# Layer 1 of a two-layer decoder trunk: the softmax of head groups 0 and 2 turned by DMA in 16-bit halves, that of groups 1 and 3 by PE transposes

## The chip, the cores and the metric

The kernel runs on one core of a Trainium2 chip. The metric is the device time of one execution in microseconds; the text compares the median of several runs. The engines are TensorE (PE; its weight loads are shown apart as PEld), VectorE (DVE), ScalarE (ACT), GpSimd (POOL) and SyncE (SP). SP computes nothing here, it issues DMAs. Every engine and every queue works through its own instructions in a fixed order, and waits on semaphores where one instruction needs the result of another engine.

## The reference

A sequence of 256 tokens of width 2048 goes through two layers and a last RMSNorm. A layer is: RMSNorm, mixer, residual add, RMSNorm, SwiGLU, residual add. Layer 0 mixes with sliding-window attention beside an mLSTM. Layer 1, the one that is changed, mixes with forgetting attention: 16 heads of 128, causal softmax with a bias made of a running sum of log forget gates. Everything is float32. Cut to what matters here:

```python
def forgetting_attention_mixer(xn, w_in, b_f, w_out):
    q, k, v, f = split_cols(xn @ w_in, FOX_SIZES)          # 3 x 2048 and 16 columns
    q, k, v = to_heads(q), to_heads(k), to_heads(v)        # 16 heads of 128
    log_f = log_sigmoid(f + b_f)
    c = cumsum(log_f, axis=1)
    def one_block(qb, cb, pb):                             # 128 queries
        s = einsum('bhqd,bhkd->bhqk', qb, k) * scale
        s = s + cb[..., None] - c[:, :, None, :]
        s = where(pb[:, None] >= k_pos[None, :], s, -inf)
        p = softmax(s, axis=-1)
        return einsum('bhqk,bhkd->bhqd', p, v)
    out = map(one_block, blocks of 128 queries)
    return concat_heads(out) @ w_out
```

## The kernel before

All weights stream from HBM once. A chunk is two 128-row blocks of up to 512 columns (512 KB). It is loaded by SP into one of four buffers `raw` (L113), rounded by ACT to a shorter float format (`hi`, L174), and DVE makes the remainder (`lo = raw - hi`, L175). There are six buffers each for `hi` and `lo`. The activations are split likewise (`xh`, `xl`, and `mh`, `ml` for the mixer's output), and each product is three matmuls: hi x hi, hi x lo, lo x hi (L205 to L207 in `gemm`, L441 to L443 in `three`). A chunk is twelve matmuls of 512 columns.

`pair_group` (L448) multiplies two 512-column groups of weights at a time in eight positions, given as (kind, pair). Kind 0 is plain: two chunks, 24 matmuls. Kind 1 is mixed: it forms sums and differences of the two weight blocks on DVE (L500 to L503), splits them (L311, L312), and needs 21 matmuls. `MIX` has the mixed positions 1, 3 and 5. The products of the mixed positions go to four PSUM banks of the pool `pm` and are put together by `combine` (L455) ahead of the last position. A callback `inner` is called there too, after `combine`; callbacks in `todo` are called at the position that stands with each (`run_due`, L185), and what they put on ACT is queued behind the latest cast of a weight chunk.

Layer 1 goes through four head groups `i` of four heads (L1053). For each, `pair_nat(i)` projects q and k, `project` makes a 512-column group of v, and `attention` (L333) does scores, bias, mask, maximum, exponential and division. The scores stand in one tile `s` of 128 x 4 heads x 384 columns: 128 columns for the first block of queries, which sees one block of keys, and 256 for the second, which sees two. `attention` ends with the division (L385) and returns the function `rest`; that is passed as `inner` to the next group's `pair_nat`, so that group i's `rest` is issued ahead of the last position of `pair_nat(i+1)`. Group 3's `rest` is called after the loop.

`rest` turns the 12 blocks of 128 x 128 so that keys lie on partitions: eight PE transposes to PSUM (L394) and two ACT copies to the tile `t0` (L395), four transposes (L398) and one DVE copy to `t1` (L399). Then come the value matmuls (L402, L403) and the split of their result into `mh` and `ml` (L412, recorded at L311 and L312). The output projection reads `mh` and `ml` as its stationary side, group after group.

For i < 3 the function `turn` (L1017) turns q and k by DMA: ACT parts float32 numbers into two planes of upper and lower 16-bit halves (L1022), SP issues four DMA transposes of 128 x 512 halves for each of q and k (L1025), and a `join` later puts the halves together again on ACT (L1030). For i = 3 q and k are turned by PE (L330).

The order of the instructions on each engine comes from a scheduler at compile time. It runs a model of the time of all engines and issues what is ready there, in the order of the program where there is a choice. On the chip that order is fixed.

The sums of x for the mixed positions of layer 1 are made in the first group's `pair_nat`, at positions 1, 3 and 6 (`sums_of_x`, L1034), in the tiles `t0` and `t1`, which the attention doesn't use yet. Layer 0's attention uses the same function `attention`, with tiles of its own pool.

Of the kernel before, what the change touches and what calls it, by code (L numbers as in the profile page):

```python
# [7 lines left out]
F32 = mybir.dt.float32  # L8
BF16 = mybir.dt.bfloat16
F32R = mybir.dt.float32r  # L10
U16 = mybir.dt.uint16
# [6 lines left out]
P = 128  # L18
D = 2048
S = 256  # L20
# [3 lines left out]
NB = 512  # L24
# [6 lines left out]
FOX_H, FD = 16, 128  # L31
# [12 lines left out]
MIX = ((0, 0), (1, 1), (0, 2), (1, 3), (0, 4), (1, 5), (0, 6), (0, 7))  # L44
MIX0 = ((0, 0), (0, 1), (0, 2), (1, 3), (0, 4), (1, 5), (0, 6), (0, 7))
# [4 lines left out]
LATER = (6, 10, 3, 5)  # L50
LATER_DOWN = (5, 6)
RAWS = 4
PARTS = (0, 3, 7, 11)


# [7 lines left out]
def trunk(  # L63
# [20 lines left out]
    nc = tc.nc  # L84

    sp_ = ctx.enter_context(tc.tile_pool(name="split", bufs=1))
    xh = sp_.tile([P, KT, S], F32R, name="xh")
    xl = sp_.tile([P, KT, S], F32R, name="xl")
# [151 lines left out]
    def whole(hi, lo, pair):  # L240
        ks = slice(2 * pair, 2 * pair + 2)
        return lambda full: nc.vector.tensor_tensor(
            out=full, in0=hi[:, ks, :].bitcast(F32), in1=lo[:, ks, :].bitcast(F32), op=ALU.add
        )

    def sums_of(pool, sh, sl, copies, full=None, tags=("tmp", "tmp"), bufs=None):
        if full is None:
            full = pool.tile([P, 2, NT, P], F32, tag=tags[0], name="full", bufs=bufs)
            copies(full.rearrange("p i t q -> p i (t q)"))
        s = pool.tile([P, 4, P], F32, tag=tags[1], name="s4", bufs=bufs)  # L250
        nc.vector.tensor_tensor(out=s[:, 0, :], in0=full[:, 0, 1, :], in1=full[:, 1, 1, :], op=ALU.add)
        nc.vector.tensor_tensor(out=s[:, 1, :], in0=s[:, 0, :], in1=full[:, 0, 0, :], op=ALU.subtract)
        nc.vector.tensor_tensor(out=s[:, 2, :], in0=full[:, 0, 0, :], in1=full[:, 0, 1, :], op=ALU.subtract)
        nc.vector.tensor_tensor(out=s[:, 3, :], in0=full[:, 1, 0, :], in1=s[:, 1, :], op=ALU.subtract)
        split_plain(sh, sl, s)
# [74 lines left out]
            nc.tensor.transpose(pt[:, i, :], s_, ident)  # L330
        nc.vector.tensor_copy(dst, pt[:, 0:m, :])

    def attention(sp, q_of, k_of, v_of, dv, scale, bias0, bias1, k_tile, sinks=None, negc=None, s_bufs=2, causal=False):  # L333
        s = sp.tile([P, 4, 3 * P], F32, tag="s", name="s", bufs=s_bufs)
        for b, cols, bias in ((0, P, bias0), (1, S, bias1)):
            pq = [pm.tile([P, 2, cols], F32, tag="pm", name=f"p{b}") for _ in range(2)]
            for j in range(4):
                nc.tensor.matmul(pq[j % 2][:, j // 2, :], q_of(j, b), k_of(j)[:, 0:cols], start=True, stop=True)  # L338
            for half in range(2):
                hs = slice(half, 4, 2)  # L340
                nc.vector.scalar_tensor_tensor(
                    out=s[:, hs, b * P : b * P + cols],
                    in0=pq[half],
                    scalar=scale,
                    in1=bias[:, hs, :],
                    op0=ALU.mult,
                    op1=ALU.add,
                )
            if causal and b == 0:
                o = s[:, :, 0:P]  # L350
                nc.gpsimd.affine_select(
                    out=o, in_=o, pattern=[[0, 4], [-1, P]], compare_op=ALU.is_ge, fill=NEG, base=0, channel_multiplier=1
                )
        parts = (slice(0, P), slice(P, 3 * P))
        mx = sm.tile([P, NT, 4], F32, tag="mx", name="mx")
        for b in range(NT):
            nc.vector.reduce_max(mx[:, b, :], s[:, :, parts[b]], axis=AX)
        neg = sm.tile([P, NT, 4], F32, tag="neg", name="neg")
        den = sm.tile([P, NT, 4], F32, tag="den", name="den")
        if sinks is not None:  # L360
            sk = sinks[:, None, :].broadcast_to([P, NT, 4])
            nc.vector.tensor_tensor(out=mx, in0=mx, in1=sk, op=ALU.max)
            nc.vector.tensor_scalar(neg, mx, -1.0, None, op0=ALU.mult)
        else:
            nc.vector.tensor_tensor(out=mx, in0=mx, in1=negc, op=ALU.subtract)
            nc.vector.scalar_tensor_tensor(
                out=neg, in0=negc, scalar=-1.0, in1=mx, op0=ALU.mult, op1=ALU.subtract
            )
        for b in range(NT):
            for j in range(4):  # L370
                e = s[:, j, parts[b]]
                nc.scalar.activation(
                    e, e, AF.Exp, bias=neg[:, b, j : j + 1], accum_out=den[:, b, j : j + 1]
                )
        if sinks is not None:
            es = sm.tile([P, NT, 4], F32, tag="es", name="es")
            nc.vector.tensor_tensor(out=es, in0=neg, in1=sk, op=ALU.add)
            nc.scalar.activation(es, es, AF.Exp)
            nc.vector.tensor_tensor(out=den, in0=den, in1=es, op=ALU.add)
        rec = sm.tile([P, NT, 4], F32, tag="rec", name="rec")  # L380
        nc.vector.reciprocal(rec, den)
        for b in range(NT):
            for j in range(4):
                e = s[:, j, parts[b]]
                nc.vector.tensor_scalar(e, e, rec[:, b, j : j + 1], None, op0=ALU.mult)  # L385
        def rest():
            t0 = sp.tile([P, 4, S], F32, tag="t0", name="t0", bufs=1)
            t1 = sp.tile([P, 4, P], F32, tag="t1", name="t1", bufs=1)
            for half in range(2):
                pt = pm.tile([P, 2, S], F32, tag="pm", name="pp")  # L390
                for jj in range(2):
                    j = 2 * half + jj
                    for b in range(NT):
                        nc.tensor.transpose(pt[:, jj, b * P : (b + 1) * P], s[:, j, b * P : (b + 1) * P], ident)  # L394
                nc.scalar.copy(t0[:, 2 * half : 2 * half + 2, :], pt)  # L395
            pt = pm.tile([P, 4, P], F32, tag="pm", name="pp1")
            for j in range(4):
                nc.tensor.transpose(pt[:, j, :], s[:, j, 2 * P : 3 * P], ident)  # L398
            nc.vector.tensor_copy(t1, pt)  # L399

            def pv(po, j):
                nc.tensor.matmul(po, v_of(j, 0), t0[:, j, :], start=True, stop=False)  # L402
                nc.tensor.matmul(po[:, P : 2 * P], v_of(j, 1), t1[:, j, :], start=False, stop=True)  # L403

            per = P // dv
            for q in range(0, 4 // per, 2):
                po = pm.tile([P, 2, S], F32, tag="pm", name="po")
                for i in range(2):
                    for u in range(per):
                        pv(po[u * dv : (u + 1) * dv, i, :], (q + i) * per + u)  # L410
                ks = slice(k_tile + q, k_tile + q + 2)
                split_plain(mh[:, ks, :], ml[:, ks, :], po)  # L412

        return rest

    def spare_halves():
        return [
# [245 lines left out]
    with tc.tile_pool(name="ev", bufs=1) as ev:  # L663
# [17 lines left out]
        sx = [hs_[:, i, :, :, :] for i in range(2)]  # L681
# [4 lines left out]
        vs = sw.tile([P, NT, nk], F32, name="vs")  # L686
# [75 lines left out]
        pu = pm.tile([P, NB], F32, tag="pm", name="pu")  # L762
# [77 lines left out]
        with tc.tile_pool(name="mp", bufs=1) as mp:  # L840
# [20 lines left out]
            c = pair_even(OFF_QM, OFF_KM, MIXQ)  # L861
# [35 lines left out]
            c = pair_even(OFF_OM, OFF_VM, MIXV)  # L897
# [62 lines left out]
    with tc.tile_pool(name="od", bufs=1) as od:  # L960
        sx = [od.tile([P, NX, 4, P], F32R, name=f"sx{i}") for i in range(2)]
# [70 lines left out]
            return join  # L1032

        def sums_of_x(j, pair):  # L1034
            return lambda: sums_of(od, sx[0][:, j, :, :], sx[1][:, j, :, :], whole(xh, xl, pair), tags=("t0", "t1"))

        todo = [(p, sums_of_x(j, pair)) for p, j, pair in [(1, 1, 3), (3, 2, 5), (6, 0, 1)]]

# [5 lines left out]
        def pair_nat(c0, c1, todo=(), order=MIX, inner=None):  # L1044
            plain, c = pair_group(od, 0, x_of, sums_x, [(wi1, c0), (wi1, c1)], order, todo, halves, inner)
            for m in range(2):
                for t in range(NT):
                    o = c[:, 2 * m + t, :]
                    nc.vector.tensor_tensor(out=o, in0=plain[m][t], in1=o, op=ALU.add)
            return c  # L1050

        rest, vs = None, []
        for i in range(4):  # L1053
            qt = od.tile([P, 4, S], F32, tag="qt", name="qtf")
            kt = od.tile([P, 4, S], F32, tag="kt", name="ktf")
            c = pair_nat(i * NB, FOX_H * FD + i * NB, todo if i == 0 else (), MIX if i else MIX0, rest)
            for a in range(2 * NT):
                nc.scalar.mul(c[:, a, :], c[:, a, :], r1[:, a % NT : a % NT + 1])
            for m, dst in enumerate((qt, kt)):
# [21 lines left out]
            def v_of(j, b, i=i, vn=vs[i]):  # L1081
                if i == 3 and j >= 2:
                    return vtail[:, b, (j - 2) * FD : (j - 1) * FD]
                return vn[:, b, j * FD : (j + 1) * FD]
# [11 lines left out]
                negc=negc[:, :, 4 * i : 4 * i + 4],  # L1096
                s_bufs=1,
                causal=i < 3,
            )
        rest()  # L1100


# [74 lines left out]
```

## Time and profile before

| | us |
|---|---|
| median of 3 runs | 2098.47 |
| lowest and highest | 2097.71, 2098.72 |
| the profiled execution, its time | 2098.21 |
| the profiled execution, its span | 2096.5 |
| softmax of group 0 divided (L385), start | 1145.73 |
| softmax of group 2 divided (L385), start | 1284.10 |

The span goes from the first to the last instruction of the profiled execution; positions in microseconds are counted from its start. The granted clock of TensorE is 0.998 of full speed. A row of the timeline gives start, length, engine, line, operation, output and input tiles, shape and count; in square brackets stands the idle time of the engine just before and what ended it. A row of a line's view gives the least, the median and the greatest length in nanoseconds, then the first and the last start.

### The profile page before, as it was taken

To read this page: it belongs to the slowest core of one execution; us is meant where nothing else is said; L and a number is where in the kernel's file an instruction comes from. 1 tells how busy PE (TensorE), PEld (TensorE's weight loads), DVE (VectorE), ACT (ScalarE), POOL (GpSimd) and SP (SyncE) were. 2 spreads that over 40 slices of the span, in tenths; PEclk is the share of its full clock that TensorE was granted. 3 is DMA by queue.
4 is the path that set the end of the run, shared out by engine and by line. 5 is a ranking of instruction groups with operands and counts; after the bars stand their busy time and mean duration, and the time that the engine had idled before them with its cause. 6 is when DMAs were issued, how large, how long until landed. Compare 5 with 4: busy or idle time off the path is not lost.

```text
span 2096.5 us, 27042 instructions
## 1 busy us (share of the span) xinstructions
PE 2079.4 (99%) x9559; PEld 1727.5 (82%) x9559; DVE 1831.4 (87%) x2416; ACT 1348.6 (64%) x1709; POOL 40.2 (2%) x68
## 2 busy tenths in 40 slices
PE   8999999999999999999999999999999999999998
PEld 7888888888888888888888888888888888888886
DVE  5688868999999998999898778679999999999994
ACT  6665559665567655766676666587655667456753
POOL 2000000000000000000000000000000000000000
PEclk9999999999999999999999999999999999999999
DMA  7455558666566666666576756486756567666663
GB/s 243 141 181 181 201 147 277 229 199 213 199 197 228 220 205 215 206 217 203 183 212 211 236 160 195 151 264 214 223 190 223 194 199 246 206 202 207 222 198 136
DMA packets 290600, 428.31 MB, mean 204 GB/s; under 512 B 89016, under 2 KB 97312, under 8 KB 290336
## 3 DMA queue, kind: packets, MB, share of 16 engines
q1 hardware_dynamic: 288896, 421.27, 63.3%
q0 software_dynamic: 1520, 5.30, 0.8%
q8 instruction: 75, 1.23, 0.2%
q14 instruction: 61, 0.50, 0.1%
q10 hardware_dynamic: 48, 0.02, 0.0%
HBM read 406.05 MB, written 2.11 MB: 195 GB/s over the span
## 4 chain that ended last, share of the span: by engine, by line
PE 98%; ACT 1%; DMA 1%; issue 0%; DVE 0%; DVEq 0%; POOLq 0%; POOL 0%; ACTq 0%
PE acc L442 21%; PE acc L443 21%; PE acc L441 21%; PE acc L205 6%; PE acc L206 6%; PE acc L207 6%; PE prod L442 5%; PE prod L441 5%; PE prod L443 5%; PE p L338 1%; PE po L402 1%; DMA raw<-in_w_in_odd_dram 0%; PE pp L394 0%; PE ptm L330 0%; PE po L403 0%
## 5 line engine op out<-in xcount | busy, mean ns | idle before, releaser
L174 ACT CAST hi<-raw 128x1024 fp32r<-128x1024 f32 (+3 forms) x655 | 665.8, 1031 | 463.6 <-PE acc L443 286.3
L175 DVE TENSOR_TENSOR lo<-raw,hi 128x1024 fp32r<-128x1024 f32 (+3 forms) x655 | 775.0, 1198 | 144.4 <-ACT hi L174 142.2
L442 PE MATMUL acc<-lo,xh 128*128 128x512 f32 x1254 | 488.8, 390 | 0.5 <-DVE lo L175 0.5
L441 PE MATMUL acc<-hi,xh 128*128 128x512 f32 x1254 | 486.5, 390 | 0.0
L443 PE MATMUL acc<-hi,xl 128*128 128x512 f32 x1254 | 484.9, 390 | 0.0
L442 PEld LDWEIGHTS acc<-lo,xh 128*128 128x128 f32 x1254 | 235.5, 188 | 50.1 <-DVE lo L175 1.2
L443 PEld LDWEIGHTS acc<-hi,xl 128*128 128x128 f32 x1254 | 235.4, 188 | 48.8
L441 PEld LDWEIGHTS acc<-hi,xh 128*128 128x128 f32 x1254 | 235.2, 188 | 48.7 <-issue 0.2
L442 PE MATMUL acc<-lo,mh 128*128 128x512 f32 x437 | 169.7, 389 | 0.0
L443 PE MATMUL acc<-hi,ml 128*128 128x512 f32 x437 | 168.2, 389 | 0.0
L441 PE MATMUL acc<-hi,mh 128*128 128x512 f32 x437 | 167.9, 389 | 0.0
L311 ACT CAST hi<-raw 128x512 fp32r<-128x512 f32 x109 | 67.6, 621 | 93.9 <-PE acc L443 79.0
L206 PE MATMUL acc<-lo,mh 128*128 128x512 f32 x320 | 125.7, 393 | 0.0
L205 PE MATMUL acc<-hi,mh 128*128 128x512 f32 x320 | 125.2, 393 | 0.1
L207 PE MATMUL acc<-hi,ml 128*128 128x512 f32 x320 | 122.3, 393 | 0.0
L311 ACT CAST ht<-t 128x1024 fp32r<-128x1024 f32 x95 | 99.8, 1051 | 34.4 <-PE prod L443 27.8
L312 DVE TENSOR_TENSOR lt<-t,ht 128x1024 fp32r<-128x1024 f32 x95 | 115.8, 1219 | 5.3 <-ACT ht L311 5.3
L311 ACT CAST ht<-raw 128x1024 fp32r<-128x1024 f32 x95 | 99.6, 1049 | 28.3 <-PE acc L443 13.8
L312 DVE TENSOR_TENSOR lt<-raw,ht 128x1024 fp32r<-128x1024 f32 x95 | 115.8, 1219 | 1.3 <-ACT ht L311 1.3
L205 PE MATMUL acc<-hi,xh 128*128 128x512 f32 (+3 forms) x288 | 100.1, 351 | 0.9 <-ACT hi L174 0.9
L206 PE MATMUL acc<-lo,xh 128*128 128x512 f32 (+3 forms) x288 | 100.8, 351 | 0.0
L207 PE MATMUL acc<-hi,xl 128*128 128x512 f32 (+3 forms) x288 | 99.2, 349 | 0.0
(353 smaller groups left out, 3448.7 us busy)
## 6 DMA issues: line engine op xcount, KB each, us to landing
raw<-in_w_gate_dram SPq DMA_DIRECT2D x176, 512.0 KB, 4.4
raw<-in_w_up_dram SPq DMA_DIRECT2D x176, 512.0 KB, 4.6
raw<-in_w_down_dram SPq DMA_DIRECT2D x176, 512.0 KB, 5.1
raw<-in_w_in_odd_dram SPq DMA_DIRECT2D x88, 512.0 KB, 5.3
raw<-in_w_in_even_dram SPq DMA_DIRECT2D x52, 512.0 KB, 4.5
raw<-in_w_out_even_dram SPq DMA_DIRECT2D x32, 512.0 KB, 4.4
raw<-in_w_out_odd_dram SPq DMA_DIRECT2D x32, 512.0 KB, 4.3
hr<-in_w_in_even_dram SPq DMA_DIRECT2D x12, 512.0 KB, 5.3
```

Source lines behind the costliest of these rows:

```text
L174: latest[0] = nc.scalar.copy(hi[:, :, 0:n], raw[:, :, 0:n])
L175: nc.vector.tensor_tensor(out=lo[:, :, 0:n], in0=raw[:, :, 0:n], in1=hi[:, :, 0:n].bitcast(F32), op=ALU.subtract)
L205: nc.tensor.matmul(o, ah[:, ts], hi, start=(k == 0), stop=False)
L206: nc.tensor.matmul(o, ah[:, ts], lo, start=False, stop=False)
L207: nc.tensor.matmul(o, al[:, ts], hi, start=False, stop=(k == k_all - 1))
L311: nc.scalar.copy(dst_h, src)
L312: nc.vector.tensor_tensor(out=dst_l, in0=src, in1=dst_h.bitcast(F32), op=ALU.subtract)
L338: nc.tensor.matmul(pq[j % 2][:, j // 2, :], q_of(j, b), k_of(j)[:, 0:cols], start=True, stop=True)
L402: nc.tensor.matmul(po, v_of(j, 0), t0[:, j, :], start=True, stop=False)
L441: nc.tensor.matmul(o, ah, hi, start=start, stop=False)
L442: nc.tensor.matmul(o, ah, lo, start=False, stop=False)
L443: nc.tensor.matmul(o, al, hi, start=False, stop=stop)
```

## The change

In layer 1, `attention` is called with `turned` for groups 0 and 2. It then issues `turn_p` directly behind the division: ACT parts the 1536 columns of `s` into two planes of 16-bit halves in the tile `tt`, SP issues six DMA transposes of 128 x 512 halves from `tt` back into `s`, and a function `join` is returned, which puts the halves together into `tt` by two ACT copies. The join is handed to the next group's `pair_nat` as a callback at position 4 (`P_JOIN`). `rest`, still called ahead of the last position, then has only the value matmuls and their split. Groups 1 and 3 keep the PE transposes, now in a function `transpose_p`.

`t0` and `t1` become one tile `tt` of 128 x 4 x 3 x 128, in layer 0 too. The sums of x in the first group use one tile (`box`) in that same place.

```diff
+P_JOIN = 4
...
-    def sums_of(pool, sh, sl, copies, full=None, tags=("tmp", "tmp"), bufs=None):
-        if full is None:
+    def sums_of(pool, sh, sl, copies, full=None, tags=("tmp", "tmp"), bufs=None, box=None):
+        if box is not None:
+            full, s = box[:, 0:4, :].rearrange("p (i t) q -> p i t q", i=2), box[:, 4:8, :]
+            copies(full.rearrange("p i t q -> p i (t q)"))
+        elif full is None:
             full = pool.tile([P, 2, NT, P], F32, tag=tags[0], name="full", bufs=bufs)
             copies(full.rearrange("p i t q -> p i (t q)"))
-        s = pool.tile([P, 4, P], F32, tag=tags[1], name="s4", bufs=bufs)
+        if box is None:
+            s = pool.tile([P, 4, P], F32, tag=tags[1], name="s4", bufs=bufs)
...
-        def rest():
-            t0 = sp.tile([P, 4, S], F32, tag="t0", name="t0", bufs=1)
-            t1 = sp.tile([P, 4, P], F32, tag="t1", name="t1", bufs=1)
+        tt = sp.tile([P, 4, 3, P], F32, tag="tt", name="tt", bufs=1) if turned else None
+
+        def turn_p():
+            flat = tt.rearrange("p j c q -> p (j c q)")
+            pu = flat.bitcast(U16).rearrange("p (b n) -> p b n", b=2)
+            whole_s = s.rearrange("p j n -> p (j n)")
+            su = whole_s.bitcast(U16).rearrange("p (n b) -> p b n", b=2)
+            du = flat.bitcast(U16).rearrange("p (n b) -> p b n", b=2)
+            turned_s = whole_s.bitcast(U16).rearrange("p (b c q) -> p b c q", b=2, q=P)
+            for b in range(2):
+                nc.scalar.copy(pu[:, b, :], su[:, b, :])
+            for b in range(2):
+                for i in range(3):
+                    nc.sync.dma_start_transpose(
+                        turned_s[:, b, 4 * i : 4 * i + 4, :], pu[:, b, 4 * i * P : 4 * (i + 1) * P]
+                    )
+
+            def join():
+                for b in range(2):
+                    nc.scalar.copy(du[:, b, :], turned_s[:, b, :, :].rearrange("p c q -> p (c q)"))
+
+            return join
+
+        def transpose_p(tt):
+            t0 = tt[:, :, 0:2, :].rearrange("p j c q -> p j (c q)")
+            t1 = tt[:, :, 2, :]
             for half in range(2):
                 pt = pm.tile([P, 2, S], F32, tag="pm", name="pp")
...
+        def rest():
+            nonlocal tt
+            if tt is None:
+                tt = sp.tile([P, 4, 3, P], F32, tag="tt", name="tt", bufs=1)
+                transpose_p(tt)
+
             def pv(po, j):
-                nc.tensor.matmul(po, v_of(j, 0), t0[:, j, :], start=True, stop=False)
-                nc.tensor.matmul(po[:, P : 2 * P], v_of(j, 1), t1[:, j, :], start=False, stop=True)
+                nc.tensor.matmul(po, v_of(j, 0), tt[:, j, 0:2, :].rearrange("p c q -> p (c q)"), start=True, stop=False)
+                nc.tensor.matmul(po[:, P : 2 * P], v_of(j, 1), tt[:, j, 2, :], start=False, stop=True)
...
-        return rest
+        return (turn_p(), rest) if turned else rest
...
         def sums_of_x(j, pair):
-            return lambda: sums_of(od, sx[0][:, j, :, :], sx[1][:, j, :, :], whole(xh, xl, pair), tags=("t0", "t1"))
+            def make():
+                box = od.tile([P, 12, P], F32, tag="tt", name="box")
+                sums_of(od, sx[0][:, j, :, :], sx[1][:, j, :, :], whole(xh, xl, pair), box=box)
+
+            return make
...
-        rest, vs = None, []
+        rest, join_p, vs = None, None, []
...
-            c = pair_nat(i * NB, FOX_H * FD + i * NB, todo if i == 0 else (), MIX if i else MIX0, rest)
+            c = pair_nat(i * NB, FOX_H * FD + i * NB, todo if i == 0 else [(P_JOIN, join_p)] if join_p else (), MIX if i else MIX0, rest)
...
+                turned=i in (0,2),
             )
+            join_p = None
+            if i in (0,2):
+                join_p, rest = rest
```

More of the change, by code (lines that the diff above doesn't have):

```diff
@@ L331, in transpose_many, with attention @@
         nc.vector.tensor_copy(dst, pt[:, 0:m, :])
-    def attention(sp, q_of, k_of, v_of, dv, scale, bias0, bias1, k_tile, sinks=None, negc=None, s_bufs=2, causal=False):
+    def attention(
+        sp, q_of, k_of, v_of, dv, scale, bias0, bias1, k_tile, sinks=None, negc=None, s_bufs=2, causal=False, turned=False
+    ):
         s = sp.tile([P, 4, 3 * P], F32, tag="s", name="s", bufs=s_bufs)
```

## The prediction

> **What bounds the kernel now.** I read the page first, then the waits of PE, then the timeline around the four head groups of layer 1.
>
> ```profile
> span 2096.5 us, 27042 instructions
> PE 2079.4 (99%) x9559; PEld 1727.5 (82%) x9559; DVE 1831.4 (87%) x2416; ACT 1348.6 (64%) x1709; POOL 40.2 (2%) x68
> PE 98%; ACT 1%; DMA 1%; issue 0%; DVE 0%; DVEq 0%; POOLq 0%; POOL 0%; ACTq 0%
> PE pg L159 <- DMA gn<-in_norm_mix_dram: 3.8, 1, 3.8
> PE pp L394 <- DVE s L385: 1.7, 1, 1.7
> PE pt L264 <- DMA h<-in_x_dram: 1.3, 1, 1.3
> PE acc L205 <- ACT hi L174: 0.9, 1, 0.9
> PE acc L442 <- DVE lo L175: 0.5, 1, 0.5
> ```
>
> PE is the bound: 98% of the chain that ended last, and its waits in the whole span (waiter, releaser, total, times, longest) add up to 8.2 us. Only the last two, 1.4 us, are for weights that were split late, and none is for one of the existing DMA turns. So an instruction taken off PE is worth its place in PE's stream, and a stall put into that stream costs its whole length.
>
> A busy time per matmul is not that place, because matmuls overlap. The place is the distance from start to start:
>
> ```profile
> 1079.71 0.39 PE L443 MATMUL acc<-hi,xl 128*128 128x512 f32 x1
> ...
> 1084.47 0.39 PE L443 MATMUL acc<-hi,xl 128*128 128x512 f32 x1
> ```
>
> ```profile
> 1235.03 1.04 PE L394 MATMUL pp<-ident,s 128*128 128x128 f32 x8
> 1235.90 0.60 PE L398 MATMUL pp<-ident,s 128*128 128x128 f32 x4
> 1236.25 0.48 PE L441 MATMUL acc<-hi,xh 128*128 128x512 f32 x1
> 1236.57 0.40 PE L442 MATMUL acc<-lo,xh 128*128 128x512 f32 x1
> L394 PE MATMUL pp<-ident,s x64: 270/272/329, 87.2 to 1341.6; 128*128 128x128 f32 x64
> ```
>
> The first fence is a stretch of weight matmuls, the second the transposes of group 1 with the row of their durations. Between the first two rows lie 21 steps, 4.76 / 21 = 0.2267 us for a 512-column matmul whose row says 0.39. The twelve transposes of group 1 stand in one block: 1236.57 - 1235.03 - 0.227 = 1.31 us, 0.109 each, where the row of durations says 0.27.
>
> **What is removed.** Groups 0 and 2 lose twelve transposes each. There they are strewn among the weight matmuls, and the 512-column matmuls behind each are a little slower for a while, so I count whole stretches:
>
> ```profile
> 1156.73 0.39 PE L442 MATMUL acc<-lo,sx 128*128 128x512 f32 x1
> ...
> 1171.16 0.39 PE L443 MATMUL acc<-hi,xl 128*128 128x512 f32 x1
> 1171.39 0.60 PE L398 MATMUL pp<-ident,s 128*128 128x128 f32 x4
> 1171.82 0.60 PE L402 MATMUL po<-t,vn 128*128 128x256 f32 x2
> 1172.07 0.58 PE L205 MATMUL acc<-hi,xh 128*128 128x512 f32 x1
> ```
>
> ```profile
> 1285.67 0.39 PE L442 MATMUL acc<-lo,xh 128*128 128x512 f32 x1
> ...
> 1300.95 0.39 PE L443 MATMUL acc<-hi,xl 128*128 128x512 f32 x1
> 1301.18 0.60 PE L398 MATMUL pp<-ident,s 128*128 128x128 f32 x4
> 1301.62 0.60 PE L402 MATMUL po<-t,vn 128*128 128x256 f32 x2
> ```
>
> Group 0: from 1156.73 to 1171.16 there are 60 matmuls of 512 columns and eight L394 transposes: 14.43 - 59 x 0.2267 = 1.06 us. Its four L398 take 0.43 (to 1171.82): 1.49. Group 2: 64 matmuls and eight transposes in 15.28 us, 15.28 - 63 x 0.2267 = 1.00; with 0.44 for L398 1.44. Together 2.93 us. The lower bound is the block of group 1, 24 x 0.109 = 2.62, since some of the slowing belongs to the value matmuls that stay. I take 2.8, nearer to the stretches, because they are the very instructions removed.
>
> The Trainium skill, "TensorE: Matmul & The Clock Gate", Part 4, gives about 275 ns for a transpose in a kernel's context, from a 16-bit case. By that figure the removal would be 24 x 0.275 = 6.6 us and the time 2091.9; the duration row of this trace agrees with the figure, the starts say 0.11 to 0.13.
>
> Two L395 copies (ACT) and one L399 (DVE) per group go too.
>
> **What is added, per group.** Twice a copy that parts 1536 numbers into 16-bit planes, six DMA transposes of 128x512, twice a copy that joins them. The nearest rows are those of the existing turn of q and k, with 1024 numbers and transposes of the same shape:
>
> ```profile
> L1022 ACT COPY qtf<-c x6: 1031/1044/1048, 1085.3 to 1241.7; 128x1024 uint16<-128x1024 uint16 x6
> L1025 SPq DMA_TRANSPOSE c<-qtf x12: 1196/1264/1709, 1087.3 to 1246.7; - x12
> DMA to landing us min/median/max: 2.3/2.8/6.7
> L1030 ACT COPY qtf<-c x6: 1333/1360/1376, 1099.7 to 1251.0; 128x1024 uint16<-128x1024 uint16 x6
> L395 ACT COPY t<-pp x16: 567/580/606, 94.2 to 1342.0; 128x512 f32<-128x512 f32 x16
> 1145.73 1.93 DVE L385 TENSOR_SCALAR s<-s,rec 128x128 f32<-128x128 f32 x8
> 1284.10 1.92 DVE L385 TENSOR_SCALAR s<-s,rec 128x128 f32<-128x128 f32 x8
> ```
>
> Parting: at most 1.5 x 1.044 = 1.57 us, two make 3.1. Joining: 1.5 x 1.36 = 2.04, two make 4.1. ACT gets 7.2 - 1.2 = 6.0 us more per group. SP is held 6 x 1.264 = 7.6 us (10.3 at the maximum), plus up to 3.1 while it stands at the first transpose waiting for the planes. Group 0's numbers are ready at 1147.6 (1145.73 + 1.93), so planes to 1150.7, transposes to 1158.3, landed by 1161, joined about 1165.2.
>
> None of this is PE work. It hides behind the weight matmuls, if three queues bear it.
>
> *ACT*: casts of weights stand behind the copies. Its rows over the same time:
>
> ```profile
> 1158.02 1.05 ACT L174 CAST hi<-raw 128x1024 fp32r<-128x1024 f32 x1 [2.73 <-DMA raw<-in_w_in_odd_dram]
> 1160.63 1.05 ACT L174 CAST hi<-raw 128x1024 fp32r<-128x1024 f32 x1 [1.56 <-DMA raw<-in_w_in_odd_dram]
> 1170.08 1.05 ACT L174 CAST hi<-raw 128x1024 fp32r<-128x1024 f32 x1 [2.45 <-PE acc L443]
> ```
>
> 6.7 us idle in these gaps alone against 6.0 more. The last row matters most: ACT waits for PE to give back a split weight, all six are full. A weight chunk is 12 matmuls, 2.72 us, so a cast made there is used some five chunks, 13 us, later. Without that cover the delay of a cast, 3.1 us, would fall on PE.
>
> *SP*: weight loads stand behind the transposes. The last row is a view by stretches: PE, PEld, DVE, ACT and POOL busy, granted clock, DMA share, GB/s.
>
> ```profile
> 1151.09 6.72 SPq L113 DMA_DIRECT2D raw<-in_w_in_odd_dram  x5
> 1177.30 5.12 SPq L1025 DMA_TRANSPOSE c<-qtf  x4
> 1158.00:1162.00 4.00, 4.00 (x21) 3.22 (x20) 2.13 (x4) 2.42 (x3) 0.00 (x0) 1.00 0.96 312
> ```
>
> The load of 1151.09 would go at 1158.3, 7.2 us later; it is the one cast at 1158.02 and, by the count of full buffers, used by the projection at 1172.07. Landing 7 us later it is cast by about 1166.3 and subtracted on DVE soon after, some 3 us ahead of that use, which itself moves up to 1170.6. The transposes of q, from 1177.30, and as many of k hold SP for about 10.2 us today, and PE does not stop. Without the lead, 7 us would be lost. I cost this at nothing.
>
> *PE* itself: the value matmuls of group 0 now need the join. Today they start at 1171.82; the join is due at 1165.2, 6 us before. Group 2: numbers ready at 1286.0, joined by the same sum at 1303.6, 2 us after today's first value matmuls at 1301.62. PE has the output projection to do meanwhile, which needs group 2 only in its fifth chunk, four times 2.72 us after that, 1312.5. Cost 0, with 0 and 2 us per group as bounds.
>
> The Trainium skill speaks against the change here: "VectorE: DVE Perf Modes", Rules for kernel authors, says to use TensorE for a 128x128 transpose if a PSUM result will do, and The three transpose paths gives 1309 ns for one 16-bit block by DMA against 390 ns on TensorE. By that figure 24 blocks in a row would take 31 us per group in place of 7.6; the L1025 row, 1.264 us for four blocks, does not agree.
>
> **The other edits.** The tile tt in place of t0 and t1, and the box for the sums, wait for one release instead of two. DVE writes and reads the sums in order, so nothing is added there. In layer 0 the first copy of the next group's transposes may wait for L403 instead of L402, about 0.2 us; there the values come 4 us after the copies. I cost both at nothing.
>
> **Sum.** 2098.21 (the profiled run, span 2096.5) - 2.8 = 2095.4. The median shown, 2098.47, is 0.26 above that run, so the median to expect is 2095.7.
>
> **Rivals.**
>
> (B) The values wait for the join. PE works in a fixed order; if the order was laid out for an earlier join than the chip gives, PE stands in front of L402 and all weight matmuls behind it stand too. For it: the turned copies go through three queues, and the transposes reach 1.709 us instead of 1.264, 2.7 us for six. Against it: the q and k turns and no wait of PE for them. Price 1 us per group: 2095.7 + 2 = 2097.7, between 2096.5 and 2099 or so.
>
> (C) Slower: group 0's six transposes starve the weights. From 1150.7 to 1187.7 SP is held 7.6 + 10.2 us, or 20.9 if it also stands 3.1 for the planes. Of the 37 us 19.2, or 16.1, are left for loads; at 312 GB/s a 512 KB load takes 1.68 us, so 11.4, or 9.6, go out where PE uses 37 / 2.72 = 13.6: a shortfall of 2.2 to 4 chunks, 6 to 11 us. It decides once the lead in split weights is under that; the full buffers speak for 13. With the lead gone: 2095.7 + 6 to 11 = 2101.7 to 2106.7, the middle 2104.
>
> (D) Nothing is gained because DVE, 87% busy, paces the stage behind PE. Then 2098.5. Against it: PE waits for DVE 2.2 us in the whole span.
>
> (E) A transpose costs its duration row's 0.27 us: 24 x 0.27 = 6.5, so 2092.0. The starts speak against it.
>
> (F) Each DMA transpose runs to its landing before the next: 6 x (1.264 + 2.8) = 24.4 us. The joins end at 1179.2 and 1317.6, 7.4 us after 1171.82 and 5.1 after 1312.5, and PE stands as long: 2095.7 + 12.5 = 2108.2. The issue rows, four transposes in 5.12 us, speak against it. The Trainium skill, "VectorE: DVE Perf Modes", with its 1309 ns per block, would lead this way.
>
> **How the numbers follow.** The forecast has 0.62, B 0.17, C 0.12 (0.09 of it above 2102.7), D 0.05, E 0.03, F 0.01. The forecast's own range is 2095.5 to 2095.9 from the bounds 2.93 and 2.62, and 2094.9 to 2096.5 with half a microsecond or so for small waits that come or go. Taking in B and D it reaches 2099.5 and holds some 0.82; the low end is 2094.7. A measurement of this kernel tells 0.2%, 4.2 us, from no change: faster (below 2094.3) is E, 0.03; slower (above 2102.7) the main part of C and F, 0.10; the rest, 0.87, is within.
>
> **What would show it.** Right: 24 fewer L394 and L398 on PE, PE idle no longer than before between 1147 and 1180 and between 1286 and 1315, starts shifted by 1.5 and then 2.8 us. B: a wait of PE at the value matmuls for the ACT join. C: a wait of PE for L174 or L175 between 1165 and 1195, behind ACT waits for the raw weights. D: the same span with PE idle spread over many small gaps. What would make me wrong most is a different order of work after 1147, in which the mixed products or the values come before their data.

## The result, and the profile after

| | before | changed |
|---|---|---|
| median, us (20 runs each) | 2098.03 (2096.40 to 2101.17) | 2094.54 (2093.39 to 2097.76) |
| profiled execution, us | 2098.21 | 2093.74 |
| span, us | 2096.5 | 2092.0 |

The ratio is 0.9982, 95% interval 0.9976 to 0.9988: 3.5 us less in the medians. The interval lies wholly under 1, so the change is faster, by less than the 0.2% (4.2 us) that the prediction counts as a clear change. The time lies 0.16 us under 2094.7, the low end of the predicted range.

The page of the changed kernel, with the span, the busy times and the engine shares of the chain that ended last:

```profile
span 2092.0 us, 27017 instructions
PE 2075.2 (99%) x9535; PEld 1725.2 (82%) x9535; DVE 1828.6 (87%) x2414; ACT 1358.2 (65%) x1713; POOL 45.1 (2%) x68
PE 98%; ACT 1%; DMA 1%; issue 0%; DVE 0%; POOLq 0%; POOL 0%; ACTq 0%
```

PE has 24 matmuls fewer and is the bound as before. Its waits (waiter, releaser, total, times, longest):

```profile
PE pg L160 <- DMA gn<-in_norm_mix_dram: 3.7, 1, 3.7
PE pp L424 <- DVE s L392: 1.7, 1, 1.7
PE pt L269 <- DMA h<-in_x_dram: 1.4, 1, 1.4
PE acc L206 <- ACT hi L175: 0.8, 1, 0.8
PE acc L477 <- ACT hi L175: 0.2, 1, 0.2
```

They add up to 7.8 us, 8.2 before. None is for the new turn. The new work itself, in the timeline of groups 0 and 2 (start, duration, engine, line; L403 makes the planes, L406 transposes, L412 joins, L438 multiplies by the values):

```profile
1149.80 2.85 ACT L403 COPY tt<-s 128x1536 uint16<-128x1536 uint16 x2
1152.71 7.76 SPq L406 DMA_TRANSPOSE s<-tt  x6
1160.57 17.95 SPq L114 DMA_DIRECT2D raw<-in_w_in_odd_dram  x11
1161.72 3.72 ACT L412 COPY tt<-s 128x1536 uint16<-128x1536 uint16 x2 [1.39 <-issue]
1167.80 0.60 PE L438 MATMUL po<-tt,vn 128*128 128x256 f32 x2
...
1284.51 2.85 ACT L403 COPY tt<-s 128x1536 uint16<-128x1536 uint16 x2
1287.70 8.20 SPq L406 DMA_TRANSPOSE s<-tt  x6
1297.16 3.74 ACT L412 COPY tt<-s 128x1536 uint16<-128x1536 uint16 x2 [0.29 <-DMA s<-tt]
1302.42 0.60 PE L438 MATMUL po<-tt,vn 128*128 128x256 f32 x2
```

Group 0's join ends at 1161.72 + 3.72 = 1165.44, 2.4 us ahead of the first value matmul; group 2's at 1300.90, 1.5 us ahead. The weight loads stand behind the six transposes on SP until 1160.57, and PE does not wait for them.

So PE waits for nothing that was added. To see where the 4.5 us between the two profiles come from, compare the starts of the same instructions. The next three fences are timelines of PE: before, the changed kernel, and the changed kernel profiled a second time (the run `e_again` below). The four rows are a transpose and the next scores of layer 0, the first scores of layer 1's group 0, and the first values of its last group.

```profile
113.24 0.66 PE L330 MATMUL ptm<-ident,qn 128*128 128x128 f32 x4
128.41 0.93 PE L338 MATMUL p<-ks,qt 64*128 64x128 f32 x10
1126.19 1.06 PE L338 MATMUL p<-ktf,qtf 128*128 128x128 f32 x8
1342.80 0.59 PE L402 MATMUL po<-t,vn 128*128 128x256 f32 x2
```

```profile
113.44 0.66 PE L335 MATMUL ptm<-ident,qn 128*128 128x128 f32 x4
127.12 1.58 PE L345 MATMUL p<-ks,qt 64*128 64x128 f32 x16
1124.55 1.71 PE L345 MATMUL p<-ktf,qtf 128*128 128x128 f32 x11
1338.11 0.60 PE L438 MATMUL po<-tt,vn 128*128 128x256 f32 x2
```

```profile
113.03 0.66 PE L335 MATMUL ptm<-ident,qn 128*128 128x128 f32 x4
128.19 1.15 PE L345 MATMUL p<-ks,qt 64*128 64x128 f32 x12
1125.15 1.06 PE L345 MATMUL p<-ktf,qtf 128*128 128x128 f32 x8
1338.71 0.60 PE L438 MATMUL po<-tt,vn 128*128 128x256 f32 x2
```

| stretch | before | changed | changed, again |
|---|---|---|---|
| layer 0, row 1 to row 2 | 15.17 | 13.68 | 15.16 |
| layer 1, row 3 to row 4 | 216.61 | 213.56 | 213.56 |

The second line is the change: 3.05 us less, the same in both profiles of the changed kernel. PE does the same work there but for the transposes: the view by stretches counts 1062 matmuls before and 1039 in the changed kernel, 24 fewer but for one at the edge. The first line is not the change, because the same program has 13.68 in one execution and 15.16 in the next. The view by stretches (busy time of PE, PEld, DVE, ACT and POOL, granted clock, DMA share, GB/s) of before, of the changed kernel, and of the changed kernel again says why:

```profile
113.00:118.00 5.00, 5.00 (x30) 4.76 (x29) 2.69 (x4) 4.34 (x10) 0.00 (x0) 0.66 0.17 54
```

```profile
113.00:118.00 5.00, 5.00 (x45) 4.54 (x45) 2.90 (x4) 4.59 (x11) 0.00 (x0) 1.00 0.19 59
```

```profile
113.00:118.00 5.00, 5.00 (x30) 4.97 (x30) 2.51 (x3) 4.33 (x10) 0.00 (x0) 0.66 0.15 36
```

In the first and the third PE was granted 0.66 of its clock over these 5 us, and ran 30 instructions in place of 45: 0.34 x 5 = 1.7 us lost by the clock, 1.48 by the starts. The profile of before holds such a dip and the first profile of the changed kernel does not. It is the second that is unusual: of the 13 profiles of this text, ten show a half-clock stretch between 112 and 121 us, and three (the changed kernel's first profile, `e_no_turn` and `e_warm`) show none. Of the 4.5 us between the two spans, 3.05 are the change and 1.49 the dip. The other stretches nearly cancel: the changed kernel is 0.20 us longer ahead of the first row, 0.35 shorter between the second and the third, where before has a wait of 0.5 us for a split weight (L442, in the prediction's list), and 0.19 longer behind the last. The page's line of clocks shows 9 in every slice of both, because a slice is 52 us long.

The Trainium skill, "TensorE: Matmul & The Clock Gate", Part 1, What's actually happening, describes a throttle that halves TensorE's clock after an idle window, with a free-running window of 3413 ns. The trace agrees in size: 1.7 us lost at half clock is a window of 3.4 us. That an idle window starts it is not what the trace shows here: the view has PE busy for the whole of 100 to 118 us.

### The profile page after: what moved, and what is told of

The parts are those of the page before. It is cut to its first block, busy times and chain, and to the rows that moved or that the text cites. A ratio compares the mean times of both kernels' runs of the same rounds, so it can differ in the third digit from the quotient of the medians.

```text
span 2092.0 us, 27017 instructions
## 1 busy us (share of the span) xinstructions
PE 2075.2 (99%) x9535; PEld 1725.2 (82%) x9535; DVE 1828.6 (87%) x2414; ACT 1358.2 (65%) x1713; POOL 45.1 (2%) x68
## 4 chain that ended last, share of the span: by engine, by line
PE 98%; ACT 1%; DMA 1%; issue 0%; DVE 0%; POOLq 0%; POOL 0%; ACTq 0%
PE acc L477 21%; PE acc L478 21%; PE acc L479 21%; PE acc L206 6%; PE acc L207 6%; PE acc L208 6%; PE prod L478 5%; PE prod L479 5%; PE prod L477 5%; PE p L345 1%; PE po L438 1%; DMA raw<-in_w_in_odd_dram 0%; PE ptm L335 0%; PE pp L424 0%; PE po L439 0%
## 5 line engine op out<-in xcount | busy, mean ns | idle before, releaser
L206 PE MATMUL acc<-hi,mh 128*128 128x512 f32 x320 | 125.4, 393 | 0.1
L206 PE MATMUL acc<-hi,xh 128*128 128x512 f32 (+3 forms) x288 | 99.3, 348 | 0.8 <-ACT hi L175 0.8
```

The source lines that it names most:

```text
L206: nc.tensor.matmul(o, ah[:, ts], hi, start=(k == 0), stop=False)
```

## The experiments

Two theories, with the letters that the expectations use. R: PE loses the places of 24 transposes, 2.6 to 3 us, and all that is added is hidden. K: a further part of the difference between medians is the number of half-clock windows that an execution happens to hold. Against them stand the prediction's rivals, above all B (values wait for the join), C (weights starved), and that another part of the change saves time too. Each run was compared with the kernel before on the same chip; "fastest" is the fastest run of a kernel, taken as one with the fewest dips. The kernel before ran 95 times over all comparisons: median 2097.50, fastest 2096.06, 19 of the runs in a cluster of their own above 2099.7.

### The parts alone

`e_tiles_only`: the tile tt, the box and the rest of the edits, with no group turned (the diff shows this one); `e_group0` and `e_group2`: one group turned, with `(0,)` and `(2,)` in the two places.

```diff
-                turned=i in (0,2),
+                turned=i in (),
...
-            if i in (0,2):
+            if i in ():
```

> The changed kernel with no group turned: all four groups keep their PE transposes, the one tile tt and the box for the sums stay. Theory R (removal): the change gains the places of the 24 removed transposes on PE, 2.9 us by the stretches of the trace, and nothing else, so this kernel is within 0.4 us of the kernel before when the fastest runs of both are compared. Theory L (layer 0): the other edits gain in layer 0, where the changed kernel's profile is 1.2 us ahead by 130 us, so this kernel is 1.2 us faster than before. Theory K (clock): the 1.2 us are a stretch of 3 us near 115 us in which TensorE had half the clock in the profile of before; it comes in some executions of any kernel and not in others, so here it costs 1.5 us or nothing, and the fastest runs are equal.

> Only group 0 is turned. R: 1.5 us faster than before (12 transposes, 1.06 + 0.43 by the stretch of group 0), compared by the fastest runs and by the shift of the stages outside any stretch of low clock. A theory in which the gain comes from a better order of work in one group only would have 2.9 here or with group 2 alone, and nothing with the other.

> Only group 2 is turned. R: 1.44 us faster than before (1.00 + 0.44 by the stretch of group 2). Order theory: 0 or 2.9.

| | median, us | ratio, interval | fastest, us | first scores to last values, us |
|---|---|---|---|---|
| before, same chip | 2097.48 | | 2096.19 | 216.61 (profile of before) |
| e_tiles_only | 2096.97 | 0.9995, 0.9986 to 1.0004 | 2096.39 | 1341.42 - 1124.91 = 216.51 |
| e_group0 | 2098.72 | 0.9998, 0.9989 to 1.0007 | 2095.05 | 1343.48 - 1128.42 = 215.06 |
| e_group2 | 2096.28 | 0.9993, 0.9984 to 1.0002 | 2094.69 | 1343.05 - 1128.03 = 215.02 |

The last column takes the same two instructions as above, here for e_tiles_only, e_group0 and e_group2:

```profile
1124.91 1.27 PE L345 MATMUL p<-ktf,qtf 128*128 128x128 f32 x9
1341.42 0.59 PE L438 MATMUL po<-tt,vn 128*128 128x256 f32 x2
...
1128.42 0.83 PE L345 MATMUL p<-ktf,qtf 128*128 128x128 f32 x6
1343.48 0.59 PE L438 MATMUL po<-tt,vn 128*128 128x256 f32 x2
...
1128.03 1.27 PE L345 MATMUL p<-ktf,qtf 128*128 128x128 f32 x9
1343.05 0.60 PE L438 MATMUL po<-tt,vn 128*128 128x256 f32 x2
```

The other edits are worth 0.1 us, group 0's turn 1.55 and group 2's 1.59 against before, and the two add up to the whole, with one profile behind each figure. The medians alone would not have shown this: all three intervals hold 1. e_group0's eleven runs fall into five at 2095.05 to 2096.89 and six at 2098.7 to 2099.2, and its median happens to stand in the upper cluster.

### The added work taken away

`e_no_turn` leaves out the planes and the DMA transposes; the join is one plain copy of the untransposed softmax, so the values of groups 0 and 2 are not the reference's.

```diff
-            for b in range(2):
-                nc.scalar.copy(pu[:, b, :], su[:, b, :])
-            for b in range(2):
-                for i in range(3):
-                    nc.sync.dma_start_transpose(
...
-                for b in range(2):
-                    nc.scalar.copy(du[:, b, :], turned_s[:, b, :, :].rearrange("p c q -> p (c q)"))
+                nc.scalar.copy(flat, whole_s)
```

> Groups 0 and 2 are not turned at all: the numbers go into the tile tt by one plain ACT copy at the place of the join, so the output of these heads isn't the reference's. R with the new work wholly hidden: the same time as the changed kernel, within 0.4 us. If the two part copies, six DMA transposes and two join copies per group cost something on the path, this kernel is faster than the changed one by that cost; by the rival B of the prediction 1 us per group, 2 in all.

Median 2094.63, ratio 0.9987 (0.9979 to 0.9996), fastest 2093.40; the changed kernel's fastest was 2093.39. The planes, the transposes and the second join copy cost nothing that can be seen. (PE's order is not quite the same in it, the last group's values come earlier, so whole times are compared here and not stretches.)

### How thin the cover is

`e_dma_twice` issues each of the new transposes twice. `e_join6` issues the join at a later position.

```diff
-                    nc.sync.dma_start_transpose(
-                        turned_s[:, b, 4 * i : 4 * i + 4, :], pu[:, b, 4 * i * P : 4 * (i + 1) * P]
-                    )
+                    for _ in range(2):
+                        nc.sync.dma_start_transpose(
+                            turned_s[:, b, 4 * i : 4 * i + 4, :], pu[:, b, 4 * i * P : 4 * (i + 1) * P]
+                        )
```

> The changed kernel with each of the twelve DMA transposes done twice: SP is held 15 us per group instead of 7.7 and the join comes 7.7 us later. Hidden work (R): within 0.5 us of the changed kernel by the fastest runs, since the full buffers hold 13 us of split weights. Rival C: the shortfall of weights grows by 7.7 us of loads, PE waits for the split weights or for the join, 3 to 8 us slower than the changed kernel.

Median 2116.07, ratio 1.0091 (1.0077 to 1.0105): 21.5 us above the changed kernel, far more than the 8 us that the rival allowed. The waits of PE in it (the lines are one further down than in the changed kernel):

```profile
PE po L439 <- ACT tt L413: 8.0, 1, 8.0
PE acc L206 <- ACT hi L175: 3.7, 2, 2.9
PE p L345 <- ACT ktf L1067: 2.0, 1, 2.0
PE po L440 <- DVE tt L430: 1.1, 1, 1.1
```

and its SP and ACT timeline around group 2:

```profile
1298.09 17.73 SPq L407 DMA_TRANSPOSE s<-tt  x11
1315.92 1.04 SPq L114 DMA_DIRECT2D raw<-in_w_out_odd_dram  x2
...
1318.30 11.98 SPq L114 DMA_DIRECT2D raw<-in_w_out_odd_dram  x6
1320.61 1.04 ACT L175 CAST hi<-raw 128x1024 fp32r<-128x1024 f32 x1 [9.40 <-DMA raw<-in_w_out_odd_dram]
...
1322.93 3.65 ACT L413 COPY tt<-s 128x1536 uint16<-128x1536 uint16 x2
```

Both rivals of the prediction at once: from 1298.09 to 1318.30 the transposes hold SP for 18.9 us, ACT sits 9.4 us for a raw weight that stands behind them, the join starts behind that cast and the next, 0.5 us after the last transpose landed (1322.41), and PE stands 8.0 us at the values. About 14 of the 21.5 us are these waits (14.8 less the 0.8 of L206 that the changed kernel has too). Around them the clock is low: 0.72 of full speed over 1174 to 1180 and over 1198 to 1204, 0.57 over 1322 to 1330. By an estimate from the clock in stretches of 2 us, with the time in which PE stands still left out, that is another 4 to 5 us; the rest was not traced. The experiment does a little more than hold SP for longer: a second transpose into the same place waits for the first to land (3.6 us of waits on SP in all).

```diff
-P_JOIN = 4
+P_JOIN = 6
```

> The join of both turned groups is issued at position 6 of the pieces in place of 4; nothing else differs from the changed kernel. The join ended 2.4 us (group 0) and 1.5 us (group 2) before the first value matmul. Theory M (the cover is that thin, and PE's order is fixed): two positions later the join ends after the place of the values, PE waits at L438 for tt, 1 to 6 us per group, and the fastest run is 2 to 10 us above that of the changed kernel. Rival (the order around the values moves with the join, so that other weight matmuls stand there): no PE wait for tt, values start some us later, and the fastest run stays within 0.5 us of the changed kernel.

Median 2094.11, ratio 0.9983 (0.9974 to 0.9992), fastest 2093.40. No wait for tt. But the edit moved nothing: the scheduler made the same program of it, with the same instructions in the same order on PE, ACT, DVE, POOL and SP as the changed kernel. The join starts 16.80 us behind the start of the division (1163.48 against 1146.68), in the changed kernel 16.81 (1161.72 against 1144.91); that it reads 1.8 us later in its trace is for the most part the dip ahead of it, which has put the first scores of group 0 1.2 us later. So this is the changed kernel once more, and what a later join would do is not shown. What it does show is that the lead of group 0's join over the values varies from execution to execution: 2.4 us in the first profile, 1.8 here (1163.48 + 3.73 against 1169.01). That the cover can be used up, the doubled transposes show.

### More groups turned

`e_groups012` (the diff) and `e_groups0123` turn three and all four groups; `e_group1` turns group 1 alone, with `(1,)` in both places. With four groups a call of the last join is added ahead of the last `rest()`.

```diff
-                turned=i in (0,2),
+                turned=i in (0,1,2),
...
-            if i in (0,2):
+            if i in (0,1,2):
```

> Groups 0, 1 and 2 turned. R: the block of group 1 goes too, 1.31 us, so the fastest runs lie 1.3 us under those of the changed kernel, 4.1 under those of before (2092.1 where before has 2096.2 and the changed kernel 2093.4). If group 1's turn, which stands between the q and k turns of groups 1 and 2, starves the weights (rival C), PE waits for L175 or L176 between 1210 and 1260 and the gain is smaller or gone.

> All four groups turned, group 3's join directly ahead of its value matmuls. After group 3 only the output projection is left as cover, and it needs group 3's heads in its last two chunks, about 1346 in the trace of before. By the measured pace of the change (division to end of join 18 us) group 3's values would be ready about 1356 instead of 1343. R with the cover gone: another 1.3 us off PE, but PE waits some 8 to 10 us near 1350, so 4 to 6 us slower than before. If PE has more cover there than I count, 2090.8.

> The values of group 1 alone are turned by DMA; groups 0, 2 and 3 keep their PE transposes. Theory that the losses with groups 0, 1 and 2 turned came from the turn of group 1 itself (its planes and joins stand on ScalarE ahead of a join of k and of the split of mh, for which PE waits in a fixed order): PE waits for ktf at L345 or for mh at L477, 2 to 6 us in all, and the time is the same as before or up to 4 us above it. Rival, that it is only the density of three turns in a row (SP and ScalarE backlog handed from group to group): no such waits over 1 us here, and the time falls by the block of group 1, 1.3 us, to a fastest run near 2094.9.

| | median, us | ratio, interval | fastest, us |
|---|---|---|---|
| e_groups012 | 2102.59 | 1.0024, 1.0014 to 1.0033 | 2100.45 |
| e_groups0123 | 2109.99 | 1.0059, 1.0046 to 1.0071 | 2107.99 |
| e_group1 | 2104.53 | 1.0033, 1.0020 to 1.0046 | 2102.87 |

All three are slower than before. e_groups012 had been expected 4.1 us faster, and e_groups0123 4 to 6 us slower, where it is 12.5. Group 1 by itself loses 7 us, more than the 4 expected, so it is its own turn and not three turns in a row; e_groups012 has the same two waits as e_group1, of 4.0 and 2.3 us. With group 3 turned as well, PE also stands 6.2 us at L438 for the last join, since no weight matmuls of a next group are left to cover it. PE's waits in e_group1:

```profile
PE prod L477 <- ACT mh L316: 4.0, 1, 4.0
PE p L345 <- ACT ktf L1066: 1.8, 1, 1.8
```

Where they come from is read in the chain that ended last (start, duration, what; cut to the steps that matter):

```profile
1248.84 1.45 SPq L1061
...
1254.95 4.06 DMA raw<-in_w_in_odd_dram
...
1273.72 0.61 DVE raw L538
1274.35 0.69 ACT mh L316
1275.31 3.61 ACT s L379 x16
1278.91 0.94 ACT mh L316
1279.90 1.22 PE prod L477 x2
```

The wait of 1.8 us is for the join of k, which itself waits for k's transposes. These hold SP to 1254.33, and the weight load behind them lands at 1259.0. In the changed kernel two loads went out between q's transposes and k's, at 1244.84; here none does, with the same number of loads ahead of q's. DVE, idle for 8.9 us ahead of it, then makes the mixed weights late, ACT casts one of them just before the sixteen exponentials of the next softmax and the other just after, and PE, in a fixed order, waits for that cast. The price grows with the clock, as the view by stretches of e_group1 shows:

```profile
1276.00:1278.00 2.00, 0.00 (x0) 0.00 (x0) 1.94 (x3) 2.00 (x11) 0.00 (x0) 0.99 0.22 81
1278.00:1280.00 2.00, 0.10 (x1) 0.10 (x1) 1.02 (x6) 1.85 (x5) 0.00 (x0) 0.50 0.74 208
1280.00:1282.00 2.00, 2.00 (x5) 1.63 (x6) 2.00 (x6) 1.01 (x1) 0.00 (x0) 0.50 0.18 62
1282.00:1284.00 2.00, 2.00 (x6) 1.54 (x6) 1.38 (x2) 0.74 (x2) 0.00 (x0) 0.50 0.32 47
```

The clock falls about 2 us before the wait of 4.0 us ends at 1279.90, and PE works on at half clock until about 1284.8, which loses some 2.4 us by the same reckoning. The two waits, 5.8 us, and these 2.4 less the 1.3 of the removed block make 6.9 of the 7 us. Why the loads fall behind after group 1 and not after group 0 is not settled.

### The clock dips

`e_again` is the changed kernel, unaltered.

> The changed kernel once more, unaltered, for the size of the difference. Theory R+K (the removed transposes are worth 2.8 to 3.0 us; the rest of the difference between medians comes from the number of 3.4-us windows at half clock that an execution happens to have): the fastest run of this set lies 2.6 to 3.2 us under the fastest of the kernel before, and its median 2 to 4.5 under the median, with the runs of both kernels in clusters some 1.5 us apart. Rival (the turn saves more than the transposes' places on PE): the fastest runs differ by 3.5 us or more too.

Median 2094.95, ratio 0.9989 (0.9980 to 0.9998), 2.5 us under the median of before; the fastest runs differ by 2.29, less than expected. Its profile has a dip at 113 to 118 us and gave the third timeline above. With `e_join6`, the same program, the changed kernel has 42 runs, median 2094.54: 2.96 under the 95 of before. Six of the 42 stand in a cluster above 2097.1, with nothing from 2095.6 to 2097.1, as 19 of the 95 do. Without the upper clusters the medians are 2097.37 and 2094.46, 2.91 apart. The clusters stand 2.8 and 3.1 us apart by their medians, where 1.5 was expected.

For K speaks the mean granted clock of each run, known for 75 runs of before and for all 42:

| mean granted clock | before, runs and median | changed, runs and median |
|---|---|---|
| 0.997 | 13, 2100.00 | 6, 2097.59 |
| 0.998 | 44, 2097.48 | 24, 2094.74 |
| 0.999 | 18, 2096.62 | 12, 2093.81 |

The two profiles that fell into an upper cluster, of e_group0 (2099.00) and e_group2 (2098.55), have twice the usual time at half clock in layer 0: 6.8 us within 112 to 121 in the first, 3.4 near 91 and 3.4 near 118 in the second. So the clusters go with the clock. Whether the number of windows accounts for all of the 2.8 us is not shown.

`e_warm` adds eight matmuls without a use in layer 0, which run from 113.6 to 115.7 us in its profile, where the dip stands in others, to see whether work on PE keeps the clock up.

```diff
+        idle = pm.tile([P, NB], F32, tag="pm", name="idle")
+        for d in range(8):
+            nc.tensor.matmul(idle, xh[:, d, 0:P], xh[:, 2 * d : 2 * d + 2, :].rearrange("p k s -> p (k s)"), start=d == 0, stop=d == 7)
```

> The changed kernel with eight matmuls of 512 columns added in layer 0 near 111 us, where PE has matmuls of 4 to 256 columns on 4 partitions; nobody reads their result. Theory K says that the stretches of half clock between 112 and 120 us follow a window with too little work on PE. Then the fastest run is 1.8 us slower than the changed kernel's (8 x 0.227), but the runs lie closer together, with none or few at a mean clock of 0.997, and the median within 1 us of the fastest. If the low clock has nothing to do with the work there, the spread stays, 1.8 us higher throughout.

Median 2095.83, ratio 0.9991 (0.9982 to 1.0000), fastest 2094.50, 1.1 us above the changed kernel's in place of the 1.8 expected. Its profile has no dip, but two of its eleven runs stand in the upper cluster all the same. The changed kernel's first profile had no dip without such matmuls. That the dips can be kept away like this is not shown, and what starts them stays open.

## Why the prediction was wrong in its number and right in its mechanism

**What failed: the base of the sum.** The step "The median shown, 2098.47, is 0.26 above that run, so the median to expect is 2095.7" took the median of three runs for that of the kernel. It is 2098.03 over the twenty runs compared with the changed kernel, and 2097.50 over 95: the base stood 0.97 us too high. A base of 2097.50 less the predicted 2.8 is 2094.7, and less the 3.05 measured 2094.45; the measured median is 2094.54. The range failed with it: "half a microsecond or so for small waits that come or go" left out that executions of one and the same kernel go from 2096.06 to 2098.72, with a second cluster from 2099.73 to 2101.17. The half-clock window of 1.49 us in the profiled run had no part in the sum, but it is not the excess by itself: most of the executions profiled here have one, and one of the changed kernel with it took 2094.34, less than that kernel's median. Why the three runs stood high is not shown, as their clocks are not known.

**The removal, 2.8 between 2.62 and 2.93: a little small.** It is 3.05 by the starts, of which the other edits have 0.1, and 2.96 by the medians. Counting the stretches, 2.93, was the better of the two methods: 0.122 per transpose strewn among weight matmuls, where the block of group 1 gave 0.109. About 0.1 us per group comes from the value matmuls, which stand closer together now: group 0's took 2.64 us before (1171.82 to 1181.71, less 32 weight matmuls of 0.2267) and take 2.55 in the changed kernel (1167.80 to 1171.26, less four).

**What is added: right.** Planes 2.85 us against 3.1, joins 3.72 against 4.1, six transposes 7.76 and 8.20 against 7.6. From the start of the division to the end of the join the prediction has 19.5 us in both groups; it was 20.5 in group 0 (1144.91 to 1165.44) and 19.6 in group 2 (1281.27 to 1300.90). In group 0 the planes began 3.0 us after the division's end and not at once, because casts of weights stood ahead of them on ACT; the shorter copies and an earlier landing made up for most of it. That the join came at 1165.44, where 1165.2 had been put, is luck in part: the division itself came 0.8 us earlier.

**That it hides at no cost: right in its result, too generous in its margin.** The values were thought to be 6 us behind the join in group 0, and 2 us ahead of it in group 2 with output projection in between. In fact the value matmuls, strewn before, stand close together, and begin 2.4 and 1.5 us behind the joins. One reading was wrong without effect: the load issued at 1151.09 landed at 1155.28, and the cast at 1158.02 waited for a later one, issued at 1152.83. The first load to stand behind the transposes was the one of 1154.57, which went at 1160.57. The "13 us" of split weights did not save e_dma_twice, where the transposes held SP 18.9 us in group 2 in place of 8.2.

**The rivals.** B and C did not happen, but they are real: e_dma_twice shows both, e_group1 shows C with SP held by k's transposes. Their prices left out the clock behind the wait. D, a PE paced by DVE, is refuted by the 3.05 us; E, 0.27 us per transpose or 6.5 in all, by the same number; F, serial transposes, by six issued in 7.76 us.

## What to carry to other kernels

Where one engine is 99% busy and waits for nothing, an instruction taken off it is worth its place in the stream, measured from start to start over a whole stretch. A median of three runs is not a base for a forecast to half a microsecond where executions of one kernel spread over five. The starts of the same instructions, before and after, tell the change from that spread, and so does the clock in stretches of a few microseconds. An edit of the program is no experiment until the order of the instructions shows that it moved something. A DMA put on the queue that loads the weights cost nothing here while a microsecond or two was left; twelve more of them, about 15 us on the queue, cost 21.5.

## What the hardware showed that was not expected

- The same program loses 1.48 us or not in layer 0, by a stretch at half clock that ten of 13 profiles have; the runs of before stand in two clusters, 76 around 2097.4 and 19 from 2099.7 to 2101.2.
- In e_group1 a wait of PE of 4.0 us went with a stretch at 0.50 of the clock from 1278 to about 1284.8; 4.9 us of it came behind the wait, some 2.4 us lost.
- Six 16-bit DMA transposes of 128x512 between two places on the chip hold their queue for 7.76 us, 1.29 each; a load behind them starts only then (1160.57).
